# A gMLP mixer's output product from parts kept in DRAM, and the order of two d_ff tiles, in a two-layer encoder trunk

## The chip, the cores and the metric

The kernel runs on one core of a Trainium2 chip. The metric is device time in microseconds (us), the median over timed executions. All engines work at once and wait for each other by semaphores: TensorE (PE, with its weight loads PEld) multiplies, VectorE (DVE), ScalarE (ACT) and GpSimd (POOL) do elementwise work, and SyncE (SP) mostly issues the DMAs between DRAM and the on-chip memory. Each engine works through its own instructions in the order in which they were laid down.

## The reference

Two layers over x of 1024 positions x 1024 channels in float32. Layer A mixes by a chunked gMLP, layer B by chunked attention, and each layer ends with a gated ConvFFN of width 2816. The part that the change touches is the end of layer A's mixer and the beginning of each ConvFFN:

```
def gmlp_mixer(h, w_in, v_norm_g, w_s, b_s, w_out):
    z = gelu(h @ w_in);  u, v = split(z, 2);  v = rmsnorm(v, v_norm_g)
    s = einsum('gij,bnjgc->bnigc', masked(w_s), v) + b_s
    return (u * s) @ w_out                     # 1024x1024 @ 1024x1024
def conv_ffn(h, w_in, conv_w, conv_b, w_down):
    a = causal_conv3(h @ w_in) + conv_b
    up, gate = split(a, 2)
    return (silu(gate) * up) @ w_down
h = h + gmlp_mixer(rmsnorm(h), ...);  h = h + conv_ffn(rmsnorm(h), ...)
```

## The kernel before

Activations lie transposed: channels on the 128 partitions, positions along the free side, in two halves of 512. A float32 operand is parted by `split` (L134): ACT rounds it to a `hi` part (L137), and DVE, or POOL where the caller says so, subtracts to get the `lo` part (L138). A product of two operands is three matmuls for each 128 channels: hi*hi, lo*hi, hi*lo.

Big products use Strassen-Winograd: seven products of half-size blocks instead of eight. `LEFT` (L292) names the weight block of each of the seven, `RIGHT` (L293) the activation block; S1 to S4 and T1 to T4 are sums of blocks. `product` (L349) is one such product for one output tile: 12 matmuls of 512 columns.

**Order of instructions.** On PE it is the order of the program text. On the other engines and on SP a planner orders instructions when the kernel is built: it takes what its own model of the times says is ready, earlier text first. `tc.issue_after(x)` forces an instruction behind x on x's engine. On PE, `put_off(us, fn)` holds a step back until the PE clock of the text (`tick`, which every matmul advances) has moved by so many us.

**Mixer loop** (from L621, 108 to 209 us). Eight steps over channel groups g in the order 0, 4, 1, 5, 2, 6, 3, 7. A step loads the group's weights (`load_w`), and for both halves of the positions it computes the spatial part (`spatial`, `mix`), the product for u (`proj`), u's gelu, and the gated result. The results of groups g < 4 are the blocks B11 and B12, of g >= 4 B21 and B22. POOL forms T1 to T4 of them (L639), and L641 stores the blocks to the DRAM buffers `ga`. `out_sums` (L611), in steps 1 to 4, loads rows of w_out, forms S1 to S4 on POOL, and stores them to `da`.

**Output product** `out_a` (L655, 209 to 291 us). 28 products n: seven passes in the order 1, 2, 6, 7, 4, 5, 3, each over four output tiles m. `make` (L686) parts the operands, up to 8 items ahead of their product. `load` (L672) fetches two raw operands each time, nine items ahead. The `lo` part of every second x operand is made by POOL. `whole` (L710) adds a finished product into h, saves h, and sums its squares (`square_sum`, L215); the sum for m = 2 is POOL's. `ahead` (L741) loads the first ConvFFN weight tile at n = 21 and parts three of its blocks at n = 25 to 27.

**Norms.** After pass 4, half 0 of h is complete: `norm_first` (L298) waits 5.5 us on the PE clock, sums the squares over the partitions on PE (`rstd_rows`, tile `pm` at L239), after 2.0 us more prepares the spread of the factors over the partitions (`spread`, product at L209, tile `bc`), and then scales and parts eight tiles, with the `lo` parts on POOL. After pass 3, half 1 follows in the same way (`norm_second`, first wait 5.0 us), beside the first products of the ConvFFN.

**ConvFFN** `ffn(l, ...)` (L756), for both layers. d_ff tiles j = 0 to 21; j uses one of two PSUM places (j % 2), each with an `up` and a `gate` bank pair. `steps` (L774) is the order of products: tiles 0 and 1 by plain blocks (steps 0 to 16, step 15 being already product 1 of tile 2), then the other products of tile 2, then tile 3 onward in the order 1, 4 of the tile before, 5, 6, 2, 7, 3. `make` (L787) parts weights up to 4 steps ahead, each S block by `block_sum` (L369). Between products ACT copies intermediate sums (`keep`, L810, and L872, L885) and DVE adds them; `conv` (L812) reads a finished PSUM pair with one ACT instruction (L817) and two DVE instructions (L819). For tile 2 the second conv follows a DVE addition (L890).

Of the kernel before, what the change touches and what calls it, by code (L numbers as in the profile page):

```python
# [41 lines left out]
def f32(ap):  # L42
    return ap.bitcast(F32)
# [3 lines left out]
def trunk(ctx: ExitStack, tc: tile.TileContext, x, a_win, a_wv, a_wst, a_bs, a_wout, w_kv, w_q, w_o,  # L47
# [167 lines left out]
    def square_sum(acc, h, m, pool, cs=slice(0, H), apart=False, eng=(2,)):  # L215
# [7 lines left out]
        S.activation(sq, h, AF.Square)  # L223
# [70 lines left out]
    def new_x():  # L294
        return {n: [None] * 4 for n in ("B12", *RIGHT.values())}

# [91 lines left out]
    ga = {n: [dp.tile([P, H], F32, name=f"ga{n}{k}") for k in range(4)] for n in RIGHT.values()}  # L388
    da = {f"S{i}": dp.tile([P, 4, H], F32, name=f"dA{i}") for i in range(1, 5)}
# [230 lines left out]
    mixed, x_ = {}, {}  # L620
    for i, g in enumerate((0, 4, 1, 5, 2, 6, 3, 7)):  # L621
# [33 lines left out]
    def out_a(after, ahead):  # L655

# [5 lines left out]
        with tc.tile_pool(name="dxa", bufs=4, reuse_waits="tile") as dx:  # L662
            turn = (1, 2, 6, 7, 4, 5, 3)

            items = [(1, what, i) for what, n in (("w", (0, 1)), ("x", range(4)), ("w", (2, 3))) for i in n]
            items += [(p, what, i) for p in turn[1:] for what in "xw" for i in range(4)]
            raw, made, order, w_ = {}, [0], {}, {}
            places = cycle([new_raw] * 4 + [lambda shape: dx.tile(shape, F32, tag="raw", name="raw")] * 4)

            def load(p, what, i):  # L670
                r = next(places)([P, 2, H])
                if what == "x":  # L672
                    for j in range(2):
                        nc.sync.dma_start(r[:, j, :], ga[RIGHT[p]][i + j])
                elif LEFT[p] in da:
                    nc.sync.dma_start(r, da[LEFT[p]][:, i:i + 2, :])
                else:
                    n, k = (int(c) - 1 for c in LEFT[p][1:])
                    for j in range(2):
                        nc.sync.dma_start(r[:, j, :].rearrange("p (k c) -> p k c", c=P), a_wout[i + j + 4 * n][:, 4 * k:4 * k + 4, :])  # L680
                for j in range(2):
                    raw[p, what, i + j] = r[:, j, :]

            def make():
                n = made[0]
                made[0] += 1  # L686
                while loads and items.index(loads[0]) < n + 9:
                    load(*loads.pop(0))
                p, what, i = item = items[n]
                parts = new_y() if what == "x" else new_w()  # L690
                (x_ if what == "x" else w_)[p, i] = parts
                eng = G if what == "x" and i % 2 else V
                with tc.issue_after(order[S].ins) if order else ExitStack(), \
# [879 lines left out]
```

## Time and profile before

| | |
|---|---|
| median of 3 runs | 2159.65 us (2156.99 to 2161.71) |
| the profiled execution | 2161.34 us, of which 2159.6 us span |
| PE busy | 2130.6 us, 99% of the span |
| DVE, ACT, POOL busy | 74%, 49%, 35% |
| mean granted TensorE clock | 0.994 of full |
| DMA | 366.10 MB, mean 170 GB/s |

The span is the time from the first to the last instruction. A row of the timeline gives start and duration of one instruction, or of several alike that follow each other (the number behind x); idle time in front of it and what ended that idle time stand in brackets. Matmuls overlap in the pipeline, so their rate is read from the distances of the starts, not from their durations.

### The profile page before, as it was taken

Reading aid. Unit: us, or ns where it says so; the run is one execution under the profiler, and the core shown is the slowest. Engines: PE = TensorE matmul, PEld = TensorE weight load, DVE = VectorE, ACT = ScalarE, POOL = GpSimd, SP = SyncE. Lnnn points to the kernel's source line nnn. Section 1 sums busy time; section 2 is a strip of 40 time slices with the busy share of each in tenths; the row PEclk is TensorE's granted clock in tenths of the full one; section 3 lists DMA queues with packets and bytes.
Section 4 is the critical chain, followed back from the end, with each engine's and each line's share of the span. In section 5 each row is a group of like instructions: output and inputs, shape, how many; then the busy total and the mean of one; then the engine's idle time right before and its main releaser. Section 6 shows DMA issues by size and latency. Waiting matters only on the chain.

```text
span 2159.6 us, 28776 instructions
## 1 busy us (share of the span) xinstructions
PE 2130.6 (99%) x9944; PEld 1777.2 (82%) x9944; DVE 1591.7 (74%) x2387; ACT 1067.7 (49%) x1865; POOL 754.1 (35%) x526
## 2 busy tenths in 40 slices
PE   9999999999999999999999999899999999999998
PEld 8888878888888888878888888778878888888887
DVE  4187789888888757675777666764988888885576
ACT  6333545545455544445555555552544445454443
POOL 1085336232334212054444553351342333331020
PEclk9999999999999999999999999999999999999999
DMA  7257633454545866634444444743154444568553
GB/s 250 78 205 256 231 98 126 146 173 145 171 166 195 276 226 230 228 110 130 120 120 118 117 117 123 223 166 127 62 192 138 169 161 146 181 239 297 206 191 130
DMA packets 172113, 366.10 MB, mean 170 GB/s; under 512 B 34880, under 2 KB 35264, under 8 KB 171968
## 3 DMA queue, kind: packets, MB, share of 16 engines
q1 hardware_dynamic: 166640, 354.62, 49.9%
q10 hardware_dynamic: 5328, 9.65, 1.3%
q8 instruction: 78, 1.28, 0.3%
q14 instruction: 67, 0.55, 0.1%
HBM read 231.49 MB, written 103.28 MB: 155 GB/s over the span
## 4 chain that ended last, share of the span: by engine, by line
PE 88%; DVE 7%; DMA 2%; issue 1%; ACT 1%; POOL 0%; DVEq 0%; SPq 0%; POOLq 0%; ACTq 0%
PE up L979 9%; PE gate L979 9%; PE up L359 7%; PE up L361 7%; PE up L364 7%; PE gate L359 5%; PE gate L361 5%; PE gate L364 5%; PE vps L494 4%; PE qkv L182 4%; PE qkv L179 4%; PE qkv L186 3%; DVE wlo L138 2%; PE ups L179 1%; PE ups L182 1%
## 5 line engine op out<-in xcount | busy, mean ns | idle before, releaser
L138 DVE TENSOR_TENSOR wlo<-raw,whi 128x512 fp32r<-128x512 f32 (+1 forms) x395 | 352.4, 901 | 183.2 <-ACT whi L137 182.9
L137 ACT CAST whi<-raw 128x512 fp32r<-128x512 f32 (+1 forms) x399 | 249.2, 628 | 318.3 <-PE gate L979 200.9
L359 PE MATMUL up<-yh,whi 128*128 128x512 f32 x688 | 268.6, 390 | 3.9 <-ACT h L810 3.5
L361 PE MATMUL up<-yh,wlo 128*128 128x512 f32 x688 | 267.8, 389 | 0.0
L1245 POOL TENSOR_TENSOR pl<-p,ph 128x640 fp32r<-128x640 f32 (+4 forms) x128 | 162.2, 1268 | 190.9 <-ACT ph L1244 140.8
L833 POOL TENSOR_TENSOR h<-a 128x512 f32<-128x512 f32 x44 | 77.1, 1753 | 381.2 <-DVE a L825 381.2
L359 PE MATMUL gate<-th,whi 128*128 128x512 f32 x496 | 193.4, 390 | 0.1
L361 PE MATMUL gate<-th,wlo 128*128 128x512 f32 x496 | 193.0, 389 | 0.0
L364 PE MATMUL up<-yl,whi 128*128 128x512 f32 x688 | 183.9, 389 | 0.0
L359 PEld LDWEIGHTS up<-yh,whi 128*128 128x128 f32 x688 | 129.1, 188 | 33.4 <-ACT h L810 4.3
L138 DVE TENSOR_TENSOR yl<-raw,yh 128x512 fp32r<-128x512 f32 x172 | 145.2, 845 | 9.8 <-ACT yh L137 9.7
L364 PEld LDWEIGHTS up<-yl,whi 128*128 128x128 f32 x688 | 129.1, 188 | 26.8
L361 PEld LDWEIGHTS up<-yh,wlo 128*128 128x128 f32 x688 | 129.2, 188 | 26.5
L182 PE MATMUL qkv<-yh,wlo 128*128 128x512 f32 x336 | 134.3, 400 | 0.0
L179 PE MATMUL qkv<-yh,whi 128*128 128x512 f32 x336 | 132.6, 395 | 0.0
L364 PE MATMUL gate<-tl,whi 128*128 128x512 f32 x496 | 132.6, 389 | 0.0
L137 ACT CAST whi<-S 128x512 fp32r<-128x512 f32 x160 | 99.0, 620 | 64.6 <-PE up L364 58.2
L979 PE MATMUL up<-yl,whi 128*128 128x512 f32 (+1 forms) x312 | 120.6, 387 | 0.0
L979 PE MATMUL up<-yh,whi 128*128 128x512 f32 (+1 forms) x312 | 120.4, 386 | 0.0
L979 PE MATMUL gate<-yh,wlo 128*128 128x512 f32 (+1 forms) x312 | 120.4, 386 | 0.0
L979 PE MATMUL up<-yh,wlo 128*128 128x512 f32 (+1 forms) x312 | 120.3, 386 | 0.0
L979 PE MATMUL gate<-yh,whi 128*128 128x512 f32 (+1 forms) x312 | 120.2, 385 | 0.0
(272 smaller groups left out, 5343.0 us busy)
## 6 DMA issues: line engine op xcount, KB each, us to landing
raw<-in_f_win SPq DMA_DIRECT2D x88, 512.0 KB
gT<-h SPq DMA_DIRECT2D x88, 256.0 KB
h<-in_f_wdown SPq DMA_DIRECT2D x44, 512.0 KB
dS<-h SPq DMA_DIRECT2D x88, 256.0 KB
raw<-dS SPq DMA_DIRECT2D x40, 512.0 KB
raw<-gT SPq DMA_DIRECT2D x40, 512.0 KB
gB<-a SPq DMA_DIRECT2D x66, 256.0 KB
raw<-in_f_wdown SPq DMA_DIRECT2D x30, 512.0 KB
```

Source lines behind the costliest of these rows:

```text
L137: behind[S] = S.copy(hi, src)
L138: return eng.tensor_tensor(lo, src, f32(hi), op=ALU.subtract)
L179: nc.tensor.matmul(ps, wh[:, k, :], xs[k][0], start=k == 0, stop=False)
L182: nc.tensor.matmul(ps, wl[:, k, :], xs[k][0], start=False, stop=False)
L186: nc.tensor.matmul(ps, wh[:, k, :], xs[k][1], start=False, stop=k == last)
L359: nc.tensor.matmul(ps, wh[:, k, :], xs[k][0], start=first and k == 0, stop=False, skip_group_check=True)
L361: nc.tensor.matmul(ps, wl[:, k, :], xs[k][0], start=False, stop=False, skip_group_check=True)
L364: nc.tensor.matmul(ps, wh[:, k, :], xs[k][1], start=False, stop=k == 3, skip_group_check=True)
L494: nc.tensor.matmul(ps, a, b, start=k == i == 0, stop=k == KD - 1 and i == 2)
L833: G.tensor_tensor(B[n], x, B.get(y) if isinstance(y, str) else y, op=ALU.subtract)
L979: nc.tensor.matmul(ps[:, cs], w[:, ms], x[:, cs], start=q == i == 0 and p in (1, 6, 5, 4), stop=q == NP - 1 and i == 2, skip_group_check=True)
L1245: marks[2] = G.tensor_tensor(pl[:, :n], pf[:, :n], f32(ph[:, :n]), op=ALU.subtract)
```

## The change

1. `out_sums` forms S1 to S4 on DVE, not on POOL. S1 and S4, and in the mixer loop T1 and B22, are parted at once (`keep_parts`), and both parts go to DRAM (`split_a`) in place of the raw block.
2. `load` and `make` move out of `out_a`. The first ten items (all of pass 1, and two B21 operands of pass 2 straight from the chip) are parted before `out_a` begins. For passes 5 and 3, whose operands are S1, T1, S4 and B22, `make` only loads the two parts by DMA.
3. In `out_a` no `lo` part and no sum of squares is POOL's any more. The sums of squares are put off by 1.6 us, and h is saved after them. The first ConvFFN tile is loaded at n = 14, and four of its blocks are parted at n = 18 to 21, into buffers of the `th`/`tl` pool, which opens sooner.
4. `norm_first` waits 3.2 and 1.5 us in place of 5.5 and 2.0, and its `lo` parts are DVE's.
5. In `ffn`, the products of tiles 2 and 3 alternate; tile 2's first conv follows its product 6. In layer A, steps up to n = 3 part only 2 steps ahead, and the first parts queue behind the last square on ACT.

```
-    def square_sum(acc, h, m, pool, cs=slice(0, H), apart=False, eng=(2,)):
+    def square_sum(acc, h, m, pool, cs=slice(0, H), apart=False, eng=(2,), off=0):
...
-        (G if m in eng else V).tensor_tensor(a, a, sq, op=ALU.add)
-        if m == KD - 2 and not (apart and cs.start):
-            V.tensor_tensor(a, a, acc[1][:, cs], op=ALU.add)
+        def add():
+            (G if m in eng else V).tensor_tensor(a, a, sq, op=ALU.add)
+            if m == KD - 2 and not (apart and cs.start):
+                V.tensor_tensor(a, a, acc[1][:, cs], op=ALU.add)
+        put_off(off, add) if off else add()
...
-        for n in da:
-            nc.sync.dma_start(da[n][:, m, :], block_sum(A, n, lambda: a3.tile([P, H], F32, tag="sd", name="sd", bufs=3), G))
+        for n in ("S1", "S2", "S3", "S4"):
+            b = block_sum(A, n, lambda: a3.tile([P, H], F32, tag="sd", name="sd", bufs=3), V)
+            if n in da:
+                nc.sync.dma_start(da[n][:, m, :], b)
+            if n in ("S2", "S4"):
+                keep_parts(n if n == "S4" else "S1", m, A)
+    def keep_parts(n, k, blocks):
+        hi, b = npl.tile([P, H], F32R, tag="acc", name="hi", bufs=accs[0]), blocks[n]
+        split(hi, b.bitcast(F32R), b)
+        nc.sync.dma_start(split_a[n][k][0], f32(hi))
+        nc.sync.dma_start(split_a[n][k][1], b)
...
-        for n in (("B21", "T2", "B22", "T3", "T4") if g >= 4 else ("B11", "T1")):
+        for n in (("B21", "T2", "T3", "T4") if g >= 4 else ("B11",)):
             nc.sync.dma_start(ga[n][g % 4], B[n])
+        if 4 <= g < 7:
+            for n in ("T1", "B22"):
+                keep_parts(n, g % 4, B)
+        if g == 6:
+            last = B["B21"]
...
+        if p in (5, 3):
+            for j in range(2):
+                nc.sync.dma_start(f32(parts[j]), split_a[(RIGHT if what == "x" else LEFT)[p]][i][j])
+            return
...
+    while made[0] < 10:
+        make()
+    for n in ("T1", "B22"):
+        keep_parts(n, 3, B)
...
-                eng = G if what == "x" and i % 2 else V
...
+                    square_sum(acc[t], y, k, npl, eng=(), off=1.6 * (k < KD - 1))
                     nc.scalar.dma_start(hsave[0][m + 4 * (p in (4, 5)), :, halves[t]], y)
-                    square_sum(acc[t], y, k, npl)
...
-        if n == 21:
+        if n == 14:
             first[0] = load_tile(0, 0)
-        if n > 24:
-            parts.append(new_w())
-            split(*parts[-1], first[0][("A11", "A12", "A21")[n - 25]])
+        if 18 <= n < 22:
+            parts.append(new_t())
+            split(*parts[-1], first[0][("A11", "A12", "A21", "A22")[n - 18]])
...
-    out_a(lambda t, acc: norm_second(h, acc, C_FG, X, 5.0) if t else norm_first(h, acc, C_FG, X, (5.5, 2.0), G), ahead)
+    out_a(lambda t, acc: norm_second(h, acc, C_FG, X, 5.0) if t else norm_first(h, acc, C_FG, X, (3.2, 1.5), V), ahead)
...
-        steps += [(2, p, None) for p in (2, 5, 6, 3, 7)]
-        for j in range(3, NF):
+        steps += [(j, p, None) for j, p in ((2, 2), (2, 5), (3, 1), (2, 3), (2, 6), (3, 2), (2, 7), (3, 5), (2, 4), (3, 6), (3, 3), (3, 7))]
+        for j in range(4, NF):
...
-            split(*w, src)
+            with tc.issue_after(behind["sq"].ins) if l == 0 and n < 8 else ExitStack():
+                split(*w, src)
...
-            while len(ready) < min(n + 4, len(steps)) and (len(ready) <= plain or n >= plain - 3):
+            while len(ready) < min(n + (4 if l or n > 3 else 2), len(steps)) and (len(ready) <= plain or n >= plain - 3):
...
-            if p == 3:
+            if p == (6 if j == 2 else 3):
```

## Rows read from the trace of the kernel before

**Rows 1.** The page's first part: busy us (share of the span) xinstructions.

```profile
PE 2130.6 (99%) x9944; PEld 1777.2 (82%) x9944; DVE 1591.7 (74%) x2387; ACT 1067.7 (49%) x1865; POOL 754.1 (35%) x526
```

**Rows 2.** PE's own waits, 200 to 420 us: total us, times, longest us.

```profile
PE gate L239 <- DVE acc L228: 2.3, 1, 2.3
PE pm L239 <- DVE acc L228: 1.9, 1, 1.9
PE up L359 <- ACT h L810: 1.3, 1, 1.3
```

**Rows 3.** PE in stretches of 4 us: start:end us, length, busy (count), granted clock, DMA.

```profile
272.00:276.00 4.00, 3.44 (x15) 0.73 0.83 305
```

**Rows 4.** PE timeline, 215 to 304 us: the last four matmuls of a product.

```profile
215.85 1.07 PE L364 MATMUL ops<-yl,whi 128*128 128x512 f32 x4
218.57 1.07 PE L364 MATMUL ops<-yl,whi 128*128 128x512 f32 x4
222.87 1.08 PE L364 MATMUL ops<-yl,whi 128*128 128x512 f32 x4
...
269.12 1.07 PE L364 MATMUL ops<-yl,whi 128*128 128x512 f32 x4
275.86 1.74 PE L364 MATMUL ops<-yl,whi 128*128 128x512 f32 x4
282.89 1.07 PE L364 MATMUL ops<-yl,whi 128*128 128x512 f32 x4
...
296.49 1.07 PE L364 MATMUL up<-yl,whi 128*128 128x512 f32 x4
303.93 1.40 PE L364 MATMUL gate<-yl,whi 128*128 128x512 f32 x4
```

**Rows 5.** PE timeline, beginnings of the two ConvFFNs, tile 2 to tile 3.

```profile
367.74 1.07 PE L364 MATMUL gate<-tl,whi 128*128 128x512 f32 x4
372.06 1.07 PE L364 MATMUL up<-yl,whi 128*128 128x512 f32 x4
...
1574.98 1.07 PE L364 MATMUL gate<-tl,whi 128*128 128x512 f32 x4
1580.19 1.07 PE L364 MATMUL up<-yl,whi 128*128 128x512 f32 x4
```

**Rows 6.** PE timeline, first products of layer B's ConvFFN.

```profile
1505.13 1.07 PE L364 MATMUL up<-yl,whi 128*128 128x512 f32 x4
1508.76 1.09 PE L364 MATMUL up<-yl,whi 128*128 128x512 f32 x4
...
1515.14 1.07 PE L364 MATMUL gate<-yl,whi 128*128 128x512 f32 x4
```

**Rows 7.** ACT timeline, layer A's ConvFFN, second conv of tile 2.

```profile
368.39 1.20 ACT L817 ACTIVATE a<-gate,cc 128x1024 f32<-128x1024 f32 x1 [4.30 <-DVE gate L890]
```

**Rows 8.** Chain that ended last, around 213 us: start, us, what.

```profile
213.11 5.43 DMA raw<-gaB
```

**Rows 9.** All engines, mixer steps 1 to 4: PE, PEld, DVE, ACT, POOL, clock, DMA.

```profile
120.00:171.00 51.00, 51.00 (x258) 43.39 (x256) 46.24 (x66) 14.98 (x25) 41.80 (x29) 1.00 0.66 222
```

**Rows 10.** Groups by line, whole kernel: count, busy us, mean ns, idle before, releasers.

```profile
L374 DVE TENSOR_TENSOR S<-raw 128x512 f32<-128x512 f32 x80 | 56.8, 710 | 69.7 <-DMA raw<-in_f_win 69.6
L374 POOL TENSOR_TENSOR sd<-sr 128x512 f32<-128x512 f32 x8 | 11.7, 1461 | 8.3 <-issue 6.2 <-DMA sr<-in_a_wout 2.2
```

**Rows 11.** DVE timeline, the same instruction with POOL busy and with POOL idle.

```profile
290.37 1.18 DVE L138 TENSOR_TENSOR wlo<-raw,whi 128x512 fp32r<-128x512 f32 x1
...
294.88 0.68 DVE L138 TENSOR_TENSOR wlo<-raw,whi 128x512 fp32r<-128x512 f32 x1
```

**Rows 12.** All engines, 285 to 299.8 us, as in Rows 9.

```profile
285.00:299.80 14.80, 12.56 (x56) 10.07 (x54) 14.80 (x20) 7.48 (x14) 9.41 (x7) 1.00 0.38 125
```

**Rows 13.** DVE and ACT timeline, mixer loop, around the end of step 1.

```profile
122.25 1.18 DVE L138 TENSOR_TENSOR wlo<-raw,whi 128x512 fp32r<-128x512 f32 x1
...
131.33 0.62 ACT L137 CAST whi<-raw 128x512 fp32r<-128x512 f32 x1 [0.79 <-PE ups L186]
```

More of the change, by code (lines that the diff above doesn't have):

```diff
@@ L386, in trunk @@
     hx = dp.tile([KD, P, T], F32, name="hx")
-    ga = {n: [dp.tile([P, H], F32, name=f"ga{n}{k}") for k in range(4)] for n in RIGHT.values()}
-    da = {f"S{i}": dp.tile([P, 4, H], F32, name=f"dA{i}") for i in range(1, 5)}
+    ga = {n: [dp.tile([P, H], F32, name=f"ga{n}{k}") for k in range(4)] for n in ("B11", "B21", "T2", "T3", "T4")}
+    da = {n: dp.tile([P, 4, H], F32, name=f"dA{n}") for n in ("S2", "S3")}
+    split_a = {n: [dp.tile([2, P, H], F32, name=f"gs{n}{k}") for k in range(4)] for n in ("T1", "B22", "S1", "S4")}
     open_psum(H, 4)
@@ L639, in trunk, with load_tile @@
             G.tensor_tensor(B[n], B[x], B[y], op=ALU.subtract)
-        for n in (("B21", "T2", "B22", "T3", "T4") if g >= 4 else ("B11", "T1")):
+        for n in (("B21", "T2", "T3", "T4") if g >= 4 else ("B11",)):
             nc.sync.dma_start(ga[n][g % 4], B[n])
-    catch_up()
+        if 4 <= g < 7:
[3 more added lines that the diff above has]
+            last = B["B21"]
+    catch_up()
+    def load_tile(l, j):
+        raw = [new_raw([P, KD, P]) for _ in range(2)]
+        for i in range(2):
+            behind["load"] = nc.sync.dma_start(raw[i], f_win[l, i * NF + j])
+        flat = [r.rearrange("p k c -> p (k c)") for r in raw]
+        return {f"A{i + 1}{k + 1}": flat[i][:, halves[k]] for i in range(2) for k in range(2)}
@@ new lines, in trunk @@
+    turn = (1, 2, 6, 7, 4, 5, 3)
+    items = [(1, what, i) for what, n in (("w", (0, 1)), ("x", range(4)), ("w", (2, 3))) for i in n] + [(2, "x", 2), (2, "x", 3)]
+    items += [i for i in [(p, what, i) for p in turn[1:] for what in "xw" for i in range(4)] if i not in items]
+    raw, made, order, x_, w_ = {(2, "x", 2): last, (2, "x", 3): B["B21"]}, [0], {}, {}, {}
+    loads = [i for i in items[:8] if i[2] % 2 == 0] + [(2, "x", 0), (2, "w", 0), (2, "w", 2)]
+    loads += [(p, what, i) for p in turn[2:5] for what, i in (("x", 0), ("w", 0), ("x", 2), ("w", 2))]
@@ new lines, in trunk, with load @@
+    places = [new_raw] * 4
+    def load(p, what, i):
+        r = places[0]([P, 2, H])
+        places.append(places.pop(0))
+        if what == "x":
+            for j in range(2):
+                nc.sync.dma_start(r[:, j, :], ga[RIGHT[p]][i + j])
+        elif LEFT[p] in da:
+            nc.sync.dma_start(r, da[LEFT[p]][:, i:i + 2, :])
+        else:
+            n, k = (int(c) - 1 for c in LEFT[p][1:])
+            for j in range(2):
+                nc.sync.dma_start(r[:, j, :].rearrange("p (k c) -> p k c", c=P), a_wout[i + j + 4 * n][:, 4 * k:4 * k + 4, :])
+        for j in range(2):
+            raw[p, what, i + j] = r[:, j, :]
@@ new lines, in make @@
+    def make():
+        n = made[0]
+        made[0] += 1
+        while loads and items.index(loads[0]) < n + 9:
+            load(*loads.pop(0))
+        p, what, i = item = items[n]
+        parts = new_y() if what == "x" else new_w()
+        (x_ if what == "x" else w_)[p, i] = parts
+        if p in (5, 3):
+            for j in range(2):
+                nc.sync.dma_start(f32(parts[j]), split_a[(RIGHT if what == "x" else LEFT)[p]][i][j])
+            return
+        with tc.issue_after(order[S].ins) if order else ExitStack(), \
+                tc.issue_after(order[V].ins) if order else ExitStack():
+            order[V] = split(*parts, raw.pop(item))
+        order[S] = behind[S]
@@ L662, in out_a @@
         with tc.tile_pool(name="dxa", bufs=4, reuse_waits="tile") as dx:
[L663 to L691, printed above, removed]
-                eng = G if what == "x" and i % 2 else V
-                with tc.issue_after(order[S].ins) if order else ExitStack(), \
-                        tc.issue_after(order[V].ins) if order and eng is V else ExitStack():
-                    lo = split(*parts, raw.pop(item), eng)
-                order[S] = behind[S]
-                if eng is V:
-                    order[V] = lo
-            loads = [i for i in items if i[2] % 2 == 0]
-            loads[4:] = [(p, what, i) for p in turn[1:] for what, i in (("x", 0), ("w", 0), ("x", 2), ("w", 2))]
+            places[:] = [lambda shape: dx.tile(shape, F32, tag="raw", name="raw")] * 4 + [new_raw] * 4
             acc = [[], []]
@@ L760, in ffn @@
         open_places()
-        left = ExitStack()
-        tpool["p"] = left.enter_context(tc.tile_pool(name=f"tp{l}", bufs=12, reuse_waits="tile"))
+        left = open_t(l) if not ready else tpool["ctx"]
         f = {"a": left.enter_context(tc.tile_pool(name=f"fa{l}", bufs=4, reuse_waits="tile"))}
```

9 lines of the change are left out of this document (7 added, 2 removed).

## The prediction

> **What bounds the kernel now.** The page's busy times come first: PE is busy 99% of the span [rows 1], and the change removes no matmul. All it can win is time in which PE stands still or runs at the lower clock, and some 29 us of idle time is all there is in the whole span. So the second view is PE's own waits, cut to the stretch that the change touches [rows 2]: two waits of 2.3 and 1.9 us for DVE's last sum of squares, one of 1.3 us for an ACT copy. The third is PE's timeline, read by the distance between the last matmuls of neighbouring products, since those durations overlap. The undisturbed distance is 218.57 - 215.85 = 2.72 us [rows 4]. Against it stand five places.
>
> A. Start of pass 2: 222.87 - 218.57 = 4.30, so 1.58 us lost.
> B. First norm sum: 275.86 - 269.12 = 6.74, and the two products and the spread after it take 282.89 - 275.86 = 7.03.
> C. Second norm sum: 303.93 - 296.49 = 7.44 [rows 4].
> D. Tile 2 to tile 3 of the ConvFFN: 4.32 in layer A and 5.21 in layer B [rows 5], so 1.60 and 2.49 lost.
>
> For B and C the measure isn't 2.72, because the sum's small matmuls and the spread are work. Layer B enters its ConvFFN without a stall and shows the fair price of both: 3.63 and 6.38 [rows 6]. So B loses 3.11 + 0.65 = 3.76 and C 3.81. [...] In all, 1.58 + 3.76 + 3.81 + 1.60 + 2.49 = 13.2 us can be won: 0.6% of the time.
>
> **The change part by part.**
>
> *Pass 2 from the chip (A).* The chain of waits shows what held pass 2: the last B21 block was stored to DRAM and read back, and the read alone took 5.43 us [rows 8]. Now this block never leaves the chip and its parting needs only ACT and DVE. I take 1.6 us, bounds 0 and 1.6. Its cover is that the other operands of pass 2 still come through DRAM, four raw places now serving eight loads; if the last came late by as much as that one read, the place would stay as it is.
>
> *First norm (B).* The sum waits for the last square, in DVE's queue behind `lo` parts for passes 5 and 3. These 16 `lo` parts go away; their operands arrive parted. POOL's ten `lo` parts in passes 1 to 4 become DVE's, at 0.68 us instead of a POOL instruction that stretches a DVE one beside it from 0.68 to 1.18 [rows 11]. The pass thus needs 8 parts, 4 additions into h and at most 2 sums, 14 x 0.68 = 9.5 us of DVE in 4 x 2.72 = 10.9 us: it fits, and from pass 4's second half on nearly only additions, sums and four ConvFFN parts remain. But the sum now stands 3.2 us behind the last product, not 5.5. Addition, square and sum, about 0.7 us each, need 2.1 of it, and hand-overs some tenths: a margin of about 0.8, so one foreign DVE instruction fits and two don't. I take 3.0 of 3.76, bounds 0 and 3.8. Passes 5 and 3 read twice as many bytes, and SP's queue holds `load_tile` behind these reads; a weight buffer comes free one pass ahead (10.9 us), a read took 5.43 under full load [rows 8], so 5.4 us cover both. For the DVE-tight passes I charge 0.5, bounds 0 and 1.5.
>
> *Second norm (C).* Before it DVE was busy 14.80 us of 14.80 beside 9.41 us of POOL [rows 12]. That POOL work becomes eight DVE parts (5.4 us), but starts earlier against the ConvFFN by the 2.3 + 0.5 us that the two waits are shortened; the weight parts of pass 3 (ACT and DVE) are gone, and the first ConvFFN products find four parts made. From the spread of the first norm to the second sum PE has 8 products and the wait of 5.0, some 21 us; DVE's list there is 8 scalings, 8 parts, 6 additions, 7 sums: 29 x 0.7 = 20. It just fits. I take 3.6 of 3.8, bounds 0 and 3.8.
>
> *Tiles 2 and 3 (D).* PE waited for an ACT copy that stood behind the conv of tile 2, and ACT stood 4.30 us waiting for DVE's addition (L890), last in a full DVE queue [rows 7]. The new order has product 4 of tile 2 two steps later with the same DVE work ahead of it: 2 x 2.72 = 5.4 us more for the queue, where 1.60 and 2.49 were missing. The conv moves one step back, which keeps 2.7 of it. Still, the copy of tile 3's product 6 again stands behind that conv. I take 1.4 and 2.0, bounds -1.0 each (the stall moves to another step and grows) and 1.6 and 2.5.
>
> *Mixer loop (a cost).* In steps 1 to 4 DVE is busy 46.24 of 51.0 us, 11.56 a step of 12.75 [rows 9]. New per step: four sums of 0.71 [rows 10], 2.8; two `lo` parts for S1 and S4, 1.4; two for T1 and B22 in every second step, 0.7: 4.9 us. Back comes what POOL's four sums of 1.46 us [rows 10] cost DVE by stretching: if three in four meet a DVE instruction with two on-chip inputs, at 0.5 each [rows 11], 1.5. That gives 11.56 + 4.9 - 1.5 = 15.0 a step, 2.2 over, about 9 us of arrears after four steps; steps 5 to 7 work them off. The weights of step 2 were ready at 123.43 and PE ended step 1 at about 131.3 [rows 13]: 7.9 us of slack. So 9.0 - 7.9 = 1.1 us of stall. Bounds: 0 with all four sums stretching (2.0 back, 6.8 of arrears), 7 with none (16.5 a step, 15 of arrears). [...]
>
> ACT's new rounding (16 casts in the mixer loop) lies beside ACT's 14.98 busy us of 51 [rows 9] and costs nothing unless one waits for a buffer.
>
> Sum: 1.6 + 3.0 + 3.6 + 1.4 + 2.0 - 0.5 - 1.1 = 10.0 us. From the profiled execution's 2161.3 that is 2151.3; it stood 1.7 above the median of the runs, so 2149.7, rounded to **2150**.
>
> **The rivals.** *Half of the waits stay* (25%). DVE is late by two or three instructions at both norm sums: nothing in the trace shows what order the planner gives, and the shortened wait leaves 0.8 us. B and C give 3.3 instead of 6.6: 2153.
>
> *The gain is eaten in the mixer loop* (18%). No relief, a stall of 7 us; B and C half, D0 and D1 half: 1.6 + 3.3 + 1.7 - 0.5 - 7 = -0.9 of gain: 2160.5. For it speaks that DVE is the fullest engine there (91%) and that its instructions stand in a fixed order, so PE's weights queue behind sums that nobody needs for 60 us.
>
> *Slower* (12%). DVE, not POOL, now waits for w_out rows, for store buffers and for POOL's T2 and T3 (a `lo` part written over T1 must wait until POOL has read it), with `vl`, the gated result and PE's weights behind it. One such wait on POOL was 2.2 us for rows [rows 10]. With one per step and no relief: 15 + 4 x 2.2 = 24 of arrears, less 7.9: 16 us of stall, and the late start takes A too. Against 8.4 to 10 of other gains that is 6 to 8 slower: 2167. It decides from about 18 us of arrears on. Against it speaks that no step showed PE waiting there before: PE was busy 51.00 of 51.00 [rows 9].
>
> **How the numbers follow.** Forecast 45%, the rivals 25, 18 and 12. The low end is all of the 13.2 and no cost, 2146, and two more for the spread of the runs: 2144. The high end reaches past the eaten gain to 2161, and leaves out the slower rival and little below. A measurement of this kernel can tell about 0.2%, 4.3 us, from no change. Faster by more: the forecast, most of the first rival and a little of the second, 0.68. Within: the rest of the first and most of the second, 0.19. Slower: 0.13.
>
> **What would show it.** Right: no PE wait for DVE's `acc` between 250 and 300 us, the granted clock at 1.00 there, the product distances at L239 near 3.6; no PE wait on L810 after tile 2 in either layer; PE's products for u still 12.75 us a step. Wrong: PE or its weight loads waiting for `wlo` or `vl` between 120 and 185 us, DVE idle on `sr`, `sd` or `g` there; a new wait at `bc`; a stall at another step of tile 3.

## The result, and the profile after

| | before | after |
|---|---|---|
| median | 2159.65 us | 2166.58 us (5 runs, 2165.16 to 2169.49) |
| profiled execution, of which span | 2161.34, 2159.6 us | 2165.16, 2163.4 us |

The ratio is 1.0036, 95% interval [1.0022, 1.0051]; a ratio here can differ by a few hundredths of a percent from the quotient of the two medians. The change made the kernel 6.9 us slower, where 9.7 us less was forecast, and the range, whose end was 2161, doesn't hold it.

The page's first part of after answers [rows 1]: the same 9944 matmuls, 40 instructions moved from POOL to DVE.

```profile
PE 2128.4 (98%) x9944; PEld 1778.1 (82%) x9944; DVE 1599.5 (74%) x2427; ACT 1067.2 (49%) x1865; POOL 685.5 (32%) x486
```

PE's own waits between 160 and 420 us (total us, times, longest us), which answer [rows 2]:

```profile
PE sp L612 <- DVE s L619: 4.6, 2, 4.2
PE gate L367 <- ACT h L855: 3.7, 1, 3.7
...
```

The two waits for `acc` are gone, as forecast. Two other waits stand there: one in the mixer loop (line L612 is the spatial product of a later step), and the old one for the ACT copy of tile 2, three times as long. The waits left out are of 0.9 us and less.

As both programs run the same number of matmuls in a fixed order, the matmul with number n of one can be laid beside number n of the other. The table is worked out that way, from the starts in the traces: how many us a kernel loses (+) or gains (-) against the profile of before, stretch by stretch. "D0" and "D1" are tile 2 to tile 4 of the two ConvFFNs, "late" all between them, "end" all behind. The lower lines belong to the experiments.

```
kernel                start  mixer    A   passes    B     C     D0    late    D1    end     sum
after                 +0.32  +6.64  -1.59 +1.13  -2.61 -3.61  +4.24  -4.05  +3.83 +0.03   +4.33
order alone           +2.24  +0.00  -0.84 -0.00  -1.54 +0.04  +4.08  -1.29  +4.63 +1.68   +8.99
old order             +2.60  +6.94  -1.59 +0.73  -2.88 -3.61  +1.25  +1.59  +1.23 +1.03   +7.29
pool sums             +0.23  +6.73  -1.27 +1.20  -2.66 -3.64  +4.29  -2.51  +4.24 +0.00   +6.62
sums behind add       +0.01  +7.31  -1.59 +1.19  -2.88 -3.64  +3.45  -4.02  +4.36 +0.04   +4.24
no S parts            -0.18  +0.00  -0.97 +2.10  -3.05 -3.63  +3.93  +0.55  +4.06 -0.04   +2.78
no T parts            +0.42  +0.00  -1.59 -0.00  -3.06 -3.61  +4.19  -5.05  +4.21 +1.38   -3.11
down sums later       -0.24  +6.89  -1.41 +2.09  -3.09 -3.60  +1.80  -1.53  +0.35 +0.79   +2.04
casts only            -0.27  +0.00  -1.59 +0.00  -2.97 -3.60  +3.84  -3.99  +3.94 +0.85   -3.79
x parts later         -0.08  +0.00  -1.59 +0.29  +1.94 -3.62  +1.49  -3.00  -0.40 +0.37   -4.60
both moves            -0.14  +8.40  -1.57 +2.55  -3.06 -3.61  -0.10  -3.57  +1.01 +0.38   +0.29
combined              +0.65  +0.79  -1.17 +0.19  -3.80 -3.61  -0.63  -2.67  -0.53 +0.58  -10.20
rows first            -0.34  +6.23  -1.59 +2.29  -0.85 -3.62  +4.43  -2.29  +3.85 -0.08   +8.02
no differences        +0.71  -0.00  -1.59 +1.26  -3.13 -3.64  +3.77  -0.22  +3.97 -0.11   +1.02
```

"Late" runs from -5 to +1.6 us among kernels that don't differ there: it is what one execution varies by, as "start" is, and as A and B of the order alone are, which changes nothing there. The profiled execution of the old order was the slowest of its twelve (2168.21 us, their median 2161.22), which its line shows. (The run with the addition earlier isn't in the table, since its stall falls on the border of two places.) The places of after alone give 6.64 - 1.59 + 1.13 - 2.61 - 3.61 + 4.24 + 3.83 = +8.0, near the 6.9 of the medians.

**What came as forecast.** PE's timeline of after, the last matmuls of a product, around the start of pass 2, the first norm and the second norm; it answers [rows 4].

```profile
220.09 1.07 PE L372 MATMUL ops<-yl,whi 128*128 128x512 f32 x4
222.81 1.07 PE L372 MATMUL ops<-yl,whi 128*128 128x512 f32 x4
...
272.90 1.07 PE L372 MATMUL ops<-yl,whi 128*128 128x512 f32 x4
274.83 0.50 PE L367 MATMUL ops<-yh,whi 128*128 128x512 f32 x1 [0.86 <-DMA whi<-gsS]
277.69 1.09 PE L372 MATMUL ops<-yl,whi 128*128 128x512 f32 x4
281.31 1.09 PE L372 MATMUL ops<-yl,whi 128*128 128x512 f32 x4
...
300.38 1.07 PE L372 MATMUL up<-yl,th 128*128 128x512 f32 x4
304.00 1.07 PE L372 MATMUL gate<-yl,th 128*128 128x512 f32 x4
```

Pass 2 begins at PE's rate (2.72 us a product). The first norm has distances of 4.79 and 3.62, where before had 6.74 and 7.03, and the second 3.62, where it had 7.44. What is left at the first norm is 0.86 us for a part that now comes from DRAM. The granted clock, 0.73 in the stretch of [rows 3], is 1.00 here.

**The stall in the mixer loop.** The table by stretch (busy us and counts of PE, PEld, DVE, ACT, POOL; granted clock; DMA), first the stretch of [rows 9], then the next 14 us:

```profile
120.00:171.00 51.00, 51.00 (x257) 43.44 (x257) 44.39 (x77) 17.78 (x32) 18.38 (x14) 1.00 0.72 240
171.00:185.00 14.00, 9.41 (x38) 7.50 (x37) 13.84 (x21) 3.94 (x7) 5.34 (x5) 0.88 0.94 332
```

DVE did 77 instructions, 11 more than before, in less busy time (44.39 against 46.24), and still PE stood. The chain of waits of after shows over what (start us, us, what):

```profile
155.67 6.80 DMA sr<-in_a_wout
...
166.25 3.51 DMA dAS<-sd
...
170.77 1.77 DVE vl L138
172.54 1.70 DVE sd L138
174.24 1.45 DVE g L138
```

DVE waits for the rows of w_out, then for a buffer of a weight sum whose store is still on its way, and then three subtractions take 1.5 to 1.8 us each. POOL's timeline has its differences T3 and T4 beside the first two, and the scaling of `spatial` (L596) beside the third:

```profile
170.26 1.74 POOL L660 TENSOR_TENSOR g<-s 128x512 f32<-128x512 f32 x1
171.96 1.74 POOL L660 TENSOR_TENSOR g<-s,g 128x512 f32<-128x512 f32 x1
173.66 1.48 POOL L596 TENSOR_TENSOR vn<-h,st 128x512 f32<-128x512 f32 x1
```

PE stands for one of the four buffers of the spatial product (`sp`), which it may write again only when DVE has read it out. DVE's last reading of that buffer and PE's next product into it, in before and then in after:

```profile
163.50 0.86 DVE L609 SCALAR_TENSOR_TENSOR s<-sp,cc,s 128x256 f32<-128x256 f32 x2
173.49 0.28 PE L602 MATMUL sp<-ws,vh 128*128 128x256 f32 x1
```

```profile
177.60 0.47 DVE L619 SCALAR_TENSOR_TENSOR s<-sp,cc,s 128x256 f32<-128x256 f32 x1
178.22 0.36 PE L612 MATMUL sp<-ws,vh 128*128 128x256 f32 x1 [4.24 <-DVE s L619]
```

In before the first of the two readings at 163.50 ends 9.5 us ahead of the product; in after it comes 14.1 us later, and the slack is gone.

**The stall at tile 2.** DVE's timeline of before in layer A, then that of after with ACT's, PE's and POOL's rows; they answer [rows 5, 7].

```profile
363.52 0.68 DVE L374 TENSOR_TENSOR S<-raw 128x512 f32<-128x512 f32 x1
...
367.01 0.68 DVE L374 TENSOR_TENSOR S<-S,raw 128x512 f32<-128x512 f32 x1
367.61 0.68 DVE L890 TENSOR_TENSOR gate<-gate,h 128x512 f32<-128x512 f32 x1
...
369.42 1.65 DVE L374 TENSOR_TENSOR S<-raw 128x512 f32<-128x512 f32 x1
```

```profile
366.98 0.69 DVE L382 TENSOR_TENSOR S<-raw 128x512 f32<-128x512 f32 x1 [2.77 <-DMA raw<-in_f_win]
...
368.79 1.41 DVE L382 TENSOR_TENSOR S<-S,raw 128x512 f32<-128x512 f32 x1
...
370.84 1.67 DVE L382 TENSOR_TENSOR S<-raw 128x512 f32<-128x512 f32 x1
372.43 1.77 DVE L138 TENSOR_TENSOR wlo<-S,whi 128x512 fp32r<-128x512 f32 x1
374.23 1.64 DVE L382 TENSOR_TENSOR S<-raw,S 128x512 f32<-128x512 f32 x1
375.80 0.68 DVE L935 TENSOR_TENSOR gate<-gate,h 128x512 f32<-128x512 f32 x1
...
376.52 1.20 ACT L862 ACTIVATE a<-gate,cc 128x1024 f32<-128x1024 f32 x1 [6.77 <-DVE gate L935]
...
378.25 0.79 PE L367 MATMUL gate<-th,whi 128*128 128x512 f32 x1 [3.72 <-ACT h L855]
381.83 1.91 PE L372 MATMUL gate<-tl,whi 128*128 128x512 f32 x4
385.63 1.07 PE L372 MATMUL up<-yl,whi 128*128 128x512 f32 x4
...
372.03 3.29 POOL L382 TENSOR_TENSOR h<-h,h 128x512 f32<-128x512 f32 x2
```

The addition (L935; in before L890) has its operands from about 369 us on, when PE ends tile 2's product 4, and runs at 375.80. All four sums of tile 4 stand ahead of it, the first waiting for a weight load, the others at 1.41 to 1.67 us beside POOL's sums of down-weights (368.35 to 375.32 us). In before two of the four stood ahead of it, and two behind. Layer B shows the same: the addition at 1583.68, behind four sums. ACT's conv stands behind the addition, the copy of tile 3's product 6 behind that, and PE behind the copy. Then the clock is low too: granted 0.65 from 376 to 380 us and 0.75 from 380 to 388 (0.50 in the first half of it, 0.99 in the second), after these 3.72 us of idle time.

```profile
376.00:380.00 4.00, 1.75 (x4) 1.47 (x5) 3.28 (x4) 2.20 (x3) 0.00 (x0) 0.65 0.18 66
380.00:388.00 8.00, 8.00 (x28) 6.33 (x28) 7.75 (x11) 4.89 (x7) 1.69 (x1) 0.75 0.41 134
```

### The profile page after: what moved, and what is told of

It is laid out like the page before. It is cut to its first block, busy times and chain, and to the rows that moved or that the text cites. A ratio compares the mean times of both kernels' runs of the same rounds, so it can differ in the third digit from the quotient of the medians.

```text
span 2163.4 us, 28792 instructions
## 1 busy us (share of the span) xinstructions
PE 2128.4 (98%) x9944; PEld 1778.1 (82%) x9944; DVE 1599.5 (74%) x2427; ACT 1067.2 (49%) x1865; POOL 685.5 (32%) x486
## 3 DMA queue, kind: packets, MB, share of 16 engines
q8 instruction: 78, 1.28, 0.3%
## 4 chain that ended last, share of the span: by engine, by line
PE 79%; DVE 8%; DMA 3%; issue 2%; ACT 1%; POOL 0%; SPq 0%; DVEq 0%; POOLq 0%; ACTq 0%
PE up L1024 9%; PE gate L1024 9%; PE up L367 6%; PE up L369 6%; PE up L372 6%; PE gate L367 5%; PE gate L369 5%; PE gate L372 5%; PE qkv L182 4%; PE qkv L179 4%; PE qkv L186 4%; PE st L1276 1%; DVE wlo L138 1%; PE po L1310 1%; PE po L1308 1%
## 5 line engine op out<-in xcount | busy, mean ns | idle before, releaser
L138 DVE TENSOR_TENSOR wlo<-raw,whi 128x512 fp32r<-128x512 f32 (+1 forms) x383 | 336.7, 888 | 182.9 <-ACT whi L137 182.7
L137 ACT CAST whi<-raw 128x512 fp32r<-128x512 f32 (+1 forms) x387 | 241.3, 629 | 305.2 <-PE gate L1024 201.7
L864 DVE SCALAR_TENSOR_TENSOR a<-gate,cc,a 128x1023 f32<-128x1023 f32 x88 | 112.3, 1277 | 12.5 <-ACT a L862 12.2
```

The lines of the kernel that those rows point to most:

```text
L137: behind[S] = S.copy(hi, src)
L138: return eng.tensor_tensor(lo, src, f32(hi), op=ALU.subtract)
L864: V.scalar_tensor_tensor(a[:, d:], src[:, :T - d], col(cw + (2 - d) * 2 * NF), a[:, d:], op0=ALU.mult, op1=ALU.add)
```

## The experiments

All ratios are to the kernel before on the same chip; line numbers are those of after where no other is said.

### Which part of the change costs

**The order alone.** The kernel before with only the new order of tiles 2 and 3:

```diff
-        steps += [(2, p, None) for p in (2, 5, 6, 3, 7)]
-        for j in range(3, NF):
+        steps += [(j, p, None) for j, p in ((2, 2), (2, 5), (3, 1), (2, 3), ..., (3, 7))]
+        for j in range(4, NF):
...
-            if p == 3:
+            if p == (6 if j == 2 else 3):
```

> The kernel before, with nothing but the new order of the products of tiles 2 and 3 in both ConvFFNs. Theory: the order itself costs 4.4 us in layer A and 3.8 in layer B, whatever comes in front of it, so about 8 us over before: 2168, with PE waiting some 4 us for the ACT copy in each layer. Rival: the order is harmless or a gain (about 3 us, as the prediction had it) and only the earlier and fuller entry into the ConvFFN of the whole change makes it stall: 2156 to 2160.

Measured: 2170.14 against 2161.80, ratio 1.0034 [1.0022, 1.0046], +8.3 us. The order loses all that the change loses, by itself: +4.08 and +4.63 in the table.

**The old order.** The changed kernel with the old order of tiles 2 and 3 (the same lines back).

> The whole change, but with the old order of tiles 2 and 3. Theory: 8 us less than the whole change, so 2158 to 2159, no longer clearly different from before; the stall in the mixer loop (about 6.6 us with its lower clock) stays. Rival: the changed entry alone makes tile 2 to 3 stall, and the time stays at 2165 or more.

Measured: 2161.22 against 2161.80, 0.9995 [0.9986, 1.0003]. So the rest of the change is worth nothing: the gains in A, B and C of some 8 us are paid back in the mixer loop (+6.94).

### The mixer loop

**Sums on POOL again.** The changed kernel, `block_sum(..., V)` in `out_sums` back to `G`.

> The whole change, but with the sums S1 to S4 of the mixer loop on POOL again; the parts for DRAM are still made in the loop. Theory: DVE loses about 11 us of work in steps 1 to 4 and no longer waits for w_out rows itself; PE's wait in step 4 (4.2 us, 6.6 with the clock) goes: 2160. Rival: the stall comes from the parts that are made in the loop (their lo parts on DVE, written over blocks that POOL still reads), and stays: 2165 or more; POOL's longer queue could even add to it.

Measured: 2168.10 against 2161.80, 1.0029 [1.0018, 1.0040]; the stall stays, +6.73. The theory that DVE's sums cause it fell. But the move isn't only a relief: POOL's sums stretch DVE again (`vl` at 163.37 takes 1.68 us and `wlo` behind it 1.78, where 0.68 is the plain length), and DVE now waits 2.4 us for POOL's differences (`g`, L660) between 120 and 178 us.

**Half of the parts left out**, once those of S1 and S4, once those of T1 and B22:

```diff
     def keep_parts(n, k, blocks):
+        if n in ("S1", "S4"):        # or ("T1", "B22")
+            for i in range(2):
+                nc.sync.dma_start(split_a[n][k][i], blocks[n])
+            return
```

> The changed kernel without the making of hi and lo of the two weight sums S1 and S4 in the mixer loop; the sum itself is stored twice instead, so bytes and stores stay, and product inputs of two of the seven products are wrong. Left out: 8 casts on ScalarE, 8 subtractions on VectorE. Theory 1 (the parts of the weight sums hold the few buffers of the sums and of hi, and with them the queues): the wait of the mixer loop, 4.2 us on PE and 6.6 in the ledger, goes: ratio about 1.0006. Theory 2 (the parts of T1 and B22 do it, stretched beside GpSimd's differences): it stays, ratio 1.003 to 1.004. Theory 3 (the loads of the output weights' rows, late on SP's queue): it stays here too, and in the run without T1's and B22's parts.

> The changed kernel without the making of hi and lo of T1 and B22 in the mixer loop and behind it; the tile itself is stored twice instead, so bytes and stores stay, and product inputs of two of the seven products are wrong. Left out: 8 casts on ScalarE, 8 subtractions on VectorE. Theory 1 (the parts of the weight sums): the wait of the mixer loop stays, ratio 1.003 to 1.004. Theory 2 (these parts): it goes, ratio about 1.0006. Theory 3 (late rows on SP's queue): stays.

Measured, against 2160.11: 2162.42 (1.0010 [0.9999, 1.0021]) and 2159.42 (0.9994 [0.9985, 1.0004]). The stall is gone in both, +0.00: each theory that put it on one kind of part fell. It takes both.

**Casts without subtractions.** In `keep_parts`, `split(...)` becomes ACT's rounding alone.

```diff
-        split(hi, b.bitcast(F32R), b)
+        S.copy(hi, b)
```

> The changed kernel with ScalarE's casts of all four kinds of parts kept in the mixer loop, and their buffers and stores, but without VectorE's subtractions (the tile itself is stored in the place of its lo part, so two of the seven products have a wrong part). Left out: 16 subtractions on VectorE. Theory 1 (VectorE's work in the loop): the wait of 4.2 us of PE for line L619 goes, ratio about 1.0006. Theory 2 (the ring of three hi buffers and ScalarE's and SP's waits for it): it stays, ratio 1.003 to 1.004.

Measured: 2160.03 against 2162.53, 0.9988 [0.9979, 0.9997], stall gone. ACT's 16 casts and the ring of three `hi` buffers alone aren't the cause. (The sums' buffers are stored sooner here too, so this run doesn't tell DVE's time from the wait for these buffers.)

**Rows first.** The changed kernel, a step's two loads of w_out rows in the text ahead of `load_w`.

> The changed kernel with the two loads of output-weight rows of a mixer step issued on SP's queue ahead of that step's load of input weights. Theory 1 (the chain begins with the rows, issued at 155.67 and there at 162.5, for which VectorE waited 1.78 us with everything behind it): the wait of 4.2 us for line L619 falls under 2, ratio 1.000 to 1.002. Theory 2 (the rows are only one of several links; the sums' buffers and GpSimd's differences hold VectorE anyway): it stays above 3, ratio 1.003 to 1.004.

Measured: 2168.85 against 2161.80, 1.0036 [1.0025, 1.0047]. The planner undid the edit: between 108 and 214 us SP issues the same transfers in the same order as in after, and the rows' 0.57 us (155.10, not 155.67) is no more than what this whole execution is ahead by ("start" in the table: -0.34 against +0.32). So this run decides nothing between its two theories. It is the changed kernel once more: the same ratio, a stall of +6.23, and the waits for the rows and for the sum's buffer at 1.23 and 1.76 us instead of 1.78 and 0.97, which is how far they differ between two executions in the same order.

**No differences.** The changed kernel without POOL's T2, T3 and T4:

```diff
+            if n in ("T2", "T3", "T4"):
+                B[n] = B["B21"]
+                continue
             B[n] = new_g()
             G.tensor_tensor(B[n], B[x], B[y], op=ALU.subtract)
```

> The changed kernel without GpSimd's differences T2, T3 and T4 in the mixer loop (B21 is stored in their place, so bytes and stores stay, and three of the seven products have a wrong input). Left out: 12 GpSimd instructions of 1.3 to 1.7 us. Theory 1 (VectorE's three parts of 1.5 to 1.8 us beside them, instead of 0.68, and the wait of T1's and B22's parts for them, are the link that turns a late queue into a stall): the wait for line L619 goes, ratio about 1.0006 or lower. Theory 2 (the chain runs over rows, sums and their buffers alone): it stays above 3 us, ratio 1.003 to 1.004.

Measured: 2160.33 against 2161.80, 0.9992 [0.9982, 1.0002], stall gone, with all of the change's own work kept. Its DVE timeline has the subtractions at their plain length, and these don't wait:

```profile
170.83 1.28 DVE L138 TENSOR_TENSOR sd<-sd,hi 128x512 fp32r<-128x512 f32 x2
172.03 0.68 DVE L138 TENSOR_TENSOR vl<-vn,vh 128x512 fp32r<-128x512 f32 x1
```

What follows for the loop: without half of DVE's new parts, or without POOL's old differences, the stall is gone, so it needs both at once. DVE's groups from 120 to 178 us (count, busy us, mean ns, idle us before them with the releasers), two of the kernel before, then those of after that are new:

```profile
L632 DVE TENSOR_TENSOR s<-s,u 128x512 f32<-128x512 f32 x9 | 13.0, 1443 | 3.0 <-ACT u L631 3.0
L138 DVE TENSOR_TENSOR wlo<-raw,whi 128x512 fp32r<-128x512 f32 x10 | 12.8, 1283 | 0.5 <-ACT whi L137 0.4
```

```profile
L138 DVE TENSOR_TENSOR wlo<-raw,whi 128x512 fp32r<-128x512 f32 x8 | 6.4, 797 | 0.0
L138 DVE TENSOR_TENSOR sd<-sd,hi 128x512 fp32r<-128x512 f32 x7 | 6.3, 894 | 1.2 <-ACT hi L137 1.2
L653 DVE TENSOR_TENSOR s<-s,u 128x512 f32<-128x512 f32 x8 | 5.5, 684 | 0.4 <-ACT u L652 0.3
...
L382 DVE TENSOR_TENSOR sd<-sr 128x512 f32<-128x512 f32 x6 | 5.0, 828 | 3.4 <-DMA sr<-in_a_wout 3.3
L138 DVE TENSOR_TENSOR g<-g,hi 128x512 fp32r<-128x512 f32 x2 | 3.3, 1650 | 0.0
L382 DVE TENSOR_TENSOR sd<-sr,sd 128x512 f32<-128x512 f32 x3 | 2.4, 791 | 1.6 <-DMA dAS<-sd 1.6
L382 DVE TENSOR_TENSOR sd<-sd,sr 128x512 f32<-128x512 f32 x3 | 2.0, 679 | 0.0
L138 DVE TENSOR_TENSOR s<-s,hi 128x512 fp32r<-128x512 f32 x2 | 1.4, 677 | 0.0
```

DVE gets back 9 x (1.44 - 0.68) + 10 x (1.28 - 0.80) = 11.6 us, since its old instructions run less beside POOL, and takes on 20.4 us for 12 sums and 11 subtractions. It was busy 52.84 us there before. That is 52.84 + 20.4 - 11.6 = 61.6 for 58 us, arrears of 3.6. On top come 6.2 us in which DVE stands: 3.4 for rows, 1.6 for a sum's buffer, 1.2 for a cast. Together that is an estimate of 9.8, about the 9.5 us of slack at the spatial buffer, while the reading came 14.1 us later. The rest is in the order. At the gated result ahead of that reading (`s<-s,u`, 160.10 in before, 168.18 in after) DVE is 8.1 us late. Then a sum and three subtractions stand ahead of the reading in after, and nothing does in before; beside POOL these four take 3.3 us more than their plain 0.68 each. Without that stretch the stall of 4.2 us would be about 1, an estimate from these rows.

So work, waits, stretching and order add up, and taking some away can bring DVE under the slack. Two things stay open: which of the two waits counts more, and how much the order does by itself, since the planner lays down another order for DVE in each of the runs without the stall, and no run holds it fixed.

### Tiles 2 and 3

**The addition earlier.** The changed kernel, tile 2's gate addition made after product 7, not after product 4.

> The whole change, with one addition of tile 2 (the gate half with its kept product 5) laid down behind product 7, as the other tiles have it, instead of behind product 4. Theory: in DVE's queue that addition stands behind three sums for tile 4, the first of which waits 2.8 us for a weight load; freed of them, the conv on ACT and the copy behind it come in time, and both stalls go (6 to 7 us with the clock in each layer): 2153 to 2155. Rival: DVE is simply in arrears there, the addition's place changes nothing, and PE still waits 3 to 4 us in each layer: 2164 to 2167.

Measured: 2166.44 against 2161.80, 1.0025 [1.0015, 1.0035]. PE now waits for the addition itself, 9.5 us in two waits. It's the queue that is late, not the addition's place in the text.

**Sums behind the addition.** Tile 4's sums are forced behind tile 2's addition on DVE:

```diff
-                    V.tensor_tensor(g2, g2, st["s5"], op=ALU.add)
+                    behind["add"] = V.tensor_tensor(g2, g2, st["s5"], op=ALU.add)
...
-            src = block_sum(...)
+            with tc.issue_after(behind["add"].ins) if j == 4 and ... else ExitStack():
+                src = block_sum(...)
```

> The changed kernel, with tile 4's sums of weights queued on VectorE behind tile 2's gate addition (both layers). Theory: the wait of 7.9 us in all for the copy of the gate half comes of VectorE's queue, where that addition stands behind sums that wait for a weight load; so the wait goes, the granted clock after it stays whole, and both entries give what the new order was to give: about 8 us off the pair, ratio to the kernel before about 0.998 (2155 us on the scale of its 2159.65). Rival: the sums, made later, are now late for tile 4's first products, and PE waits for those instead: ratio 1.001 to 1.0036. The wait of the mixer loop (PE for VectorE's line L619, 4.2 us) stays by both.

Measured: 2167.18 against 2160.11, 1.0028 [1.0017, 1.0039]: no gain. The addition is on time (369.26), and PE waits 4.0 and 4.4 us for tile 3's instead (L933 of this kernel). The theory had the queue right and fell with its price: what is behind in the queue is late by as much. The rival had the size right, and not the place (tile 4's products).

**Down sums later.** The changed kernel with POOL's first four sums of down-weights one d_ff tile later:

```diff
-                if j > 2 and j % 2 == 0:
+                if j == 5 or j > 4 and j % 2 == 0:
                     due.append(j // 2 - 2)
```

> The changed kernel with GpSimd's first four sums of down-weights (those that ran at 368.35 to 375.32 us) issued one d_ff tile later, in both layers. Theory 1 (VectorE's sums, 0.68 us alone, took 1.41 to 1.77 us beside them, and so the gate addition behind came late): VectorE gets some 4 us back, and PE's two waits for the copy behind that addition (7.9 us) shrink to under 3; ratio 1.000 to 1.0015. Theory 2 (VectorE has more to do in these 20 us than fits, with or without GpSimd): they stay above 6 us, ratio 1.003 to 1.004.

Measured: 2162.30 against 2162.53, 0.9997 [0.9986, 1.0008]. That is 0.39% off the changed kernel's ratio, for moving four POOL instructions in each layer that PE doesn't wait for. DVE's timeline shows how: from 350 to 388 us the same instructions in the same order, without POOL beside the sums. The wait for the weight load ahead of them is the same (2.73 us, 2.77 in after), so the loads that move along with POOL's sums don't explain it.

```profile
367.31 0.69 DVE L382 TENSOR_TENSOR S<-raw 128x512 f32<-128x512 f32 x1 [2.73 <-DMA raw<-in_f_win]
...
370.43 0.69 DVE L382 TENSOR_TENSOR S<-raw 128x512 f32<-128x512 f32 x1
...
371.76 0.69 DVE L382 TENSOR_TENSOR S<-raw,S 128x512 f32<-128x512 f32 x1
372.37 0.69 DVE L935 TENSOR_TENSOR gate<-gate,h 128x512 f32<-128x512 f32 x1
```

The addition comes 3.4 us sooner. PE's waits in the two layers are 2.1 us each instead of 3.7 and 4.2, and they are for tile 3's gate addition (L932), no longer for the copy. The first theory was right in the ratio and the cause, but wanted the two waits together under 3 us.

**Both moves.** Sums behind the addition and down sums later.

> The changed kernel with both moves: tile 4's sums of weights queued behind tile 2's gate addition, and GpSimd's first down-weight sums one tile later. Theory 1 (stretched VectorE work): both tile 2's and tile 3's gate additions are on time, PE's wait for them under 2 us of the 8.4; ratio 0.999 to 1.000. Theory 2 (too much work on VectorE in any order): PE still waits over 5 us in the two layers; ratio 1.002 or more.

Measured: 2159.99 against 2162.53, 0.9983 [0.9974, 0.9992]. PE still waits 2.1 us in each layer, for tile 3's gate addition, between what the two theories said. D0 and D1 are -0.10 and +1.01: even so the new order is no better than the old one.

### Versions for less time

**x parts later.** The old order; T1 and B22 stored whole and parted in `out_a`, S1 and S4 still parted in the loop.

> A correct version for less time: the changed kernel with the old order of tiles 2 and 3, and with T1 and B22 stored whole and parted in the last products, as before the change (16 parts of the weight sums stay parted in the loop). Theory: without the mixer loop's wait the ledger is 8.4 us ahead of the kernel before at tile 2, as in the run without T1's and B22's parts, and the old order loses nothing there; the 8 splits that come back cost 0 to 3 us in the passes of products 5 and 3: ratio 0.9962 to 0.9976 (2151.5 to 2154.5 us on the scale of 2159.65). Rival: the splits, now on VectorE alone, make the two norm sums late again, ratio 0.998 to 1.000.

Measured: 2155.06 against 2162.53, 0.9963 [0.9951, 0.9976]. Faster than both kernels, as the theory said. The rival was right on one place: the first norm's wait for `acc` is back with 2.3 us (B is +1.94).

**Combined.** The old order, the down sums later, T1 parted in the loop, B22 alone in the last pass:

```diff
         if 4 <= g < 7:
-            for n in ("T1", "B22"):
-                keep_parts(n, g % 4, B)
+            keep_parts("T1", g % 4, B)
...
-        if p in (5, 3):
+        if p == 5 or (p, what) == (3, "w"):
```

> A correct version for less time: the changed kernel with the old order of tiles 2 and 3, GpSimd's first down-weight sums one d_ff tile later, T1 and the weight sums parted in the mixer loop, B22 alone parted in the last product. Theory: half of the work taken out of the loop is enough for its wait of 4.2 us to go; the wait for the first norm sum (2.26 us, back in the run that parted T1 in the last products) goes again; and the old order's own waits for the copy behind tile 2's addition (2.1 and 1.4 us) go with GpSimd's sums. Ratio 0.994 to 0.9955 (2146.5 to 2150 us on the scale of 2159.65). Rivals: the loop's wait comes back with T1's parts (ratio 0.996 to 0.998); the old order's waits do not depend on GpSimd's sums (0.995 to 0.9965).

Measured: 2151.36 against 2161.83, 0.9954 [0.9940, 0.9968], the lowest ratio of all: 10.5 us under before and about 0.8% under the changed kernel's ratio. Its interval overlaps that of the x parts later, so which of these two is faster isn't shown. Between 160 and 420 us PE waits only twice, 0.6 us each, for ACT copies.

The theory held but for the rests of two waits. The loop's stall came back by 0.79 us only, with three quarters of the parts, B and C are whole, and the old order's waits behind tile 2 fell from 1.3 and 2.2 us in before to 0.6 and 1.5. That speaks for POOL's sums having a part in these too, in one execution; the ratio fits this theory and the second rival alike.

## Why the prediction was wrong

The sum had seven terms; measured, in us gained (table, first line):

| term | forecast | bounds | measured |
|---|---|---|---|
| A, start of pass 2 | 1.6 | 0 to 1.6 | 1.59 |
| B, first norm | 3.0 | 0 to 3.8 | 2.61 |
| C, second norm | 3.6 | 0 to 3.8 | 3.61 |
| DVE-tight passes | -0.5 | -1.5 to 0 | -1.13 |
| D0, D1, tiles 2 and 3 | 1.4, 2.0 | -1.0 each to 1.6, 2.5 | -4.24, -3.83 |
| mixer loop | -1.1 | -7 to 0 | -6.64 |

**A, B, C and the passes** went by their steps. The margin of 0.8 us in B sufficed: no wait for `acc` is left there.

**D is the step that failed.** It read: "5.4 us more for the queue", "with the same DVE work ahead of it". The work ahead is not the same. Product 4 ends 5.7 us later in after (its last matmuls start at 368.02, in before at 362.30), but the addition runs 8.2 us later (375.80, not 367.61). In the program text tile 4's sums come behind the addition in both kernels. The planner puts ahead what it takes to be ready first, and the addition, ready two products later, was passed by two more of these sums, with POOL's four sums beside them. The forecast even named the copy that stands behind the conv again, and gave it no price. The bound of -1.0 was not taken from a row; [rows 7] had one, ACT's 4.30 us of waiting for the same addition, which was a sign that it could come late again. Both layers passed the bound: ACT waits 6.77 us in layer A. The order alone (+8.3 us) and the old order (ratio 0.9995) show the place, and the down sums later the larger part of the reason: with DVE's four stretched instructions at 0.68 again, most of the loss goes (D0 and D1 +1.80 and +0.35). Another place in the queue is no remedy: forced behind the addition, the four sums make tile 3's late.

**The mixer loop was mis-sized, inside its bounds, and its slack was read at the wrong place.** PE did not wait there for `wlo` or `vl`, which the prediction set down as signs, but for the reading of a spatial buffer, where before has 9.5 us of slack and not the 7.9 of the weights [rows 13]. The DVE work was sized well enough: new work is 20.4 us in 4.5 steps, 4.5 a step against 4.9 charged, and the relief 2.6 a step against 1.5. The 1.5 rested on the author's estimate that three in four of POOL's sums meet a DVE instruction with two on-chip inputs; no run counts these, and the 2.6 is what the runs showed in its place. By throughput alone the slack would have covered it. What the sum left out is DVE's standing still for rows, a buffer and a cast, 6.2 us in that stretch, and what the planner puts ahead of the reading. The waits were a rival, set aside because "no step showed PE waiting there before"; but in before POOL had these waits (2.2 us for rows in [rows 10]), and there they didn't reach PE.

**The rivals.** "Eaten in the mixer loop" held in its size (7) and without its halves of B and C. "Slower" held in its sign and in part of its mechanism (DVE did wait for rows and buffers, and not for POOL's differences), at 6.6 instead of 16 us; that its 2167 lies beside the measured 2166.58 is luck, since it had no loss in D. Neither had D on the losing side, and so the range ended 5.6 us short: its high end took the loop's bound with D still winning. D at the row's 4.3 each and the loop at 7 would have given 2161.3 + 7 + 8.6 + 0.5 - 8.2 = 2169, or 2167.5 on the scale of the median.

## What to carry to other kernels

Where a queue is laid down by what is ready first, an instruction that becomes ready two steps later is passed by more look-ahead work: price a move by what newly stands ahead, and by the longest wait that the same instruction already shows, not by the time gained. Read the slack at the buffer or operand that PE would stand for. Look into the trace whether an edit moved what it was to move, since a planner can undo it. Work moved from POOL to DVE brings POOL's waits into DVE's queue (3.4 us for rows and 1.6 for a buffer here), so count these waits, not only the busy time. Where a DVE instruction on the way to PE is long (1.41 to 1.77 us instead of 0.68 here), look at POOL beside it: moving work that nobody waits for was the cheapest gain here (0.39% off the changed kernel's ratio).

## What the hardware showed

How strongly POOL's work slows DVE was more than expected. The 128x512 sums and subtractions of two on-chip inputs take 0.68 us alone and, in the rows above, 1.41 to 1.77 us beside POOL's, up to 1.1 us more. The conv step, which reads one of its inputs from PSUM, doesn't change: 1.28 us beside 1.69 us of POOL work in after, and 1.28 without (at 386.55); all 176 conv steps of after (L864) took 1.264 to 1.286 us. Why the two kinds differ isn't shown by these runs.

```profile
383.56 1.28 DVE L864 SCALAR_TENSOR_TENSOR a<-up,cc,a 128x1023 f32<-128x1023 f32 x1
```

```profile
383.12 1.69 POOL L878 TENSOR_TENSOR h<-a 128x512 f32<-128x512 f32 x1 [7.79 <-DVE a L870]
```

The other was what a wait of PE costs through the clock behind it: after 3.72 us without a matmul the granted clock was 0.65 from 376 to 380 us, 0.50 from 380 to 384 and 0.99 from 384 to 388. The last matmuls of a product start at 373.46, 381.83 and 385.63 there, 8.37 and 3.80 us apart instead of 2.72, so the one wait of 3.72 us, with the slower matmuls behind it, costs 6.7 us. A shorter wait was followed by a lower clock as well: in the run with the down sums later, PE's wait of 2.12 us in layer A ended at 382.69, and the granted clock from 380 to 388 us was 0.79, after 1.00 from 376 to 380.
